# The second layer's residual gate, spread over the partitions by a DRAM round trip instead of products on TensorE

## The chip, the cores and the metric

The kernel runs on one core of one Trainium2 chip. The metric is device time in microseconds (us) of one execution of the whole program, the median of several runs. The program is one launch; all weights, both token streams and the small parameters come from DRAM, and the output goes back there.

## The reference, cut to what matters

The model has two layers. Each normalises its tokens, multiplies them into one wide input projection that feeds three mixers (a state-space scan, differential attention, a matrix-memory LSTM), merges the three branches by sigmoid gates and projects the sum back. What the change touches is the last line of a layer: the residual gate, one number per channel that does not depend on the token.

```
shift, scale, gate = jnp.split(jax.nn.silu(c) @ w_mod + b_mod, 3, axis=-1)
...
mixed = (g[..., 0, :] * (ya @ w_branch[0]) + g[..., 1, :] * (yb @ w_branch[1])
         + g[..., 2, :] * (yc @ w_branch[2]))
return mixed @ w_out
...
x_new = x + gate[:, None] * merge(y_a, y_b, y_c, p[13])
xc_new = xc + gate_c * merge(yc_a, yc_b, yc_c, pc[13])
```

D_MODEL is 1024, and there are 256 latent tokens and 256 context tokens. The last layer has only the latent tokens to finish, since only they are returned.

## The kernel before, in words

Tokens lie on the 128 partitions in the output stage (a tile is 128 tokens by channels), so the gate must be there on every partition: the tile `gbc`, 128 x 1024. But the modulation is computed with channels on the partitions: `modc[l]` is 128 x 24 x 2, where column 16 + k of a stream holds the gate's channels 128k to 128k + 127. The kernel turns the one into the other on TensorE: for each k it takes the column `modc[l][:, 16 + k, cc]`, repeats it 128 times along the free axis as the stationary operand, and multiplies it with the identity `ident` (line 1269). The result in PSUM (`pm`, 128 x 128 for each k) is the row of 128 gate values on all partitions. ScalarE copies it out of PSUM with a factor 0.5 (line 1271). That is 8 products and 2 copies for a stream; the first layer does it for two streams, the last for one. Each of these products is two passes on TensorE, as they are float32, and so shows as two rows in the trace.

All large products are split in two parts, high and low, and computed as three products. A piece of weights (a granule, 128 x 1024, `raw`) is loaded by SP's queue (line 128), its high part `whi` is cast on ScalarE (line 117), its low part `wlo` is the difference on VectorE (line 83, by the helper `tt`), and 24 products per accumulator follow on TensorE (lines 146 to 148 with tokens on the output's partitions, lines 177 to 179 with channels there). `raw`, `whi` and `wlo` have three buffers each. A load can start when VectorE has made the `wlo` of the granule three before it, and a cast when TensorE has left the buffer of the granule three before.

The merge of a layer goes branch by branch (line 1218). The branch's result is transposed (line 1212), scaled and split in `yh` (ScalarE, line 92) and `yl` (VectorE, line 80), and then for each of four blocks of 256 channels a gate projection (`hh`, `hl`) and a branch projection (`yh`, `yl`) are computed. The third branch's result `yc` is finished late: the LSTM's last head is scaled by `riC`, which comes from a sum of squares through two small operations on GpSimd (`rs_p`, lines 89 and 83, the function `rsqrt`) and one on VectorE (line 87), and then multiplied in on VectorE (`yc`, line 80). After the merge the output projection runs: two blocks whose weights are split as above, and two whose weights were split early in the idle tiles of `yh` and `yl` (lines 1313 to 1321). The result times `gbc` is added to the residual (lines 1292 and 1293).

The second layer's modulation is computed in the first layer's merge (`mod_steps`, called from line 1199). Its last part, the gate columns, is written to `modc` by VectorE at the end of that merge (line 238).

The order of the work is set by a scheduler that works through the program by priority. `band(0)` is the most urgent (loads, splits and evacuations), then `band(1)`, then `band(2)` (the large products). SP issues its loads strictly in the order that results; so does each engine with its instructions, and an instruction that waits holds all behind it.

Of the kernel before, what the change touches and what calls it, by code (L numbers as in the profile page):

```python
# [14 lines left out]
ALU = mybir.AluOpType  # L15
# [3 lines left out]
D = 1024  # L19
P = 128  # L20
# [14 lines left out]
def hybrid_backbone_kernel(ctx: ExitStack, tc: tile.TileContext, A, out, dbg=None):  # L35
    nc = tc.nc
    V, S, G, T = nc.vector, nc.scalar, nc.gpsimd, nc.tensor
# [5 lines left out]
    @contextmanager  # L43
    def band(b):
        saved = tc.cur_priority
        tc.cur_priority = bands[b]
        yield
        bands[b] = tc.cur_priority
        tc.cur_priority = saved
# [3 lines left out]
    rows_d = ctx.enter_context(tc.tile_pool(name="rows_d", bufs=1, space=bass.MemoryType.DRAM))  # L53

    def mk(pool, shape, tag, dt=F32, bufs=1):
        if dbg is not None:
            b = 1
            for n in shape[1:]:
                b *= n
            b *= 2 if dt == BF16 else 4  # L60
            key = (pool.name, tag)
            dbg["usage"][key] = max(dbg["usage"].get(key, 0), (b + 31) // 32 * 32 * bufs)
        return pool.tile(list(shape), dt, tag=tag, name=tag, bufs=bufs)
# [4 lines left out]
    def pe():  # L68
        return mk(psum, [P, 512], "pe", bufs=PE_)

    def pm():
        return mk(psum, [P, 512], "pm", bufs=PM)
# [12 lines left out]
    def tsc(o, a, s1, op0, s2=None, op1=None, eng=None):  # L85
        if op1 is None:
            (eng or V).tensor_scalar(out=o, in0=a, scalar1=s1, scalar2=None, op0=op0)
        else:
            (eng or V).tensor_scalar(out=o, in0=a, scalar1=s1, scalar2=s2, op0=op0, op1=op1)
# [17 lines left out]
    modc = [mk(base, [P, 24, 2], "modc", bufs=2) for _ in range(depth)]  # L107
# [113 lines left out]
    def mod_mm(ps, x, k0, wm):  # L221
        for j in range(2):
            k = k0 + j
            g = k % 4

            T.matmul(
                ps[32 * g : 32 * g + 32, :], lhsT=cst[:, k, 2 - 2 * x : 34 - 2 * x], rhs=wm[:, j, :],
                start=(x == 0 and k < 4), stop=(x == 1 and k >= 4), skip_group_check=True,
            )

    def mod_tail(l, cbs, row):
        with band(2):
            pc = pacc()
            for i in range(4):
                T.matmul(pc[:, 4 * i : 4 * i + 4], lhsT=row[:, i * P : (i + 1) * P], rhs=selm, start=True, stop=True)
            for x, cb in enumerate(cbs):
                r = 16 * l + 12 + cb // 3
                tt(
                    modc[l][:, cb * 4 : cb * 4 + 4, :], pc[:, 0:16].rearrange("p (a b) -> p a b", b=4)[:, :, 2 * x : 2 * x + 2],
                    bc(pcols[:, 4 * (cb % 3) : 4 * (cb % 3) + 4, r], 2), ALU.add,  # L240
                )
# [24 lines left out]
    def mod_steps(l, cbs, pool):  # L266

        ps = None
        for x, cb in enumerate(cbs):
            with band(2):  # L270
                ps = ps or pe()
                for k0 in range(0, KT, 2):
                    wm = mk(pool, [P, 2, 512], "wm", bufs=4)
                    with band(0):
                        nc.sync.dma_start(
                            wm, A["w_mod"][l][k0 * P : (k0 + 2) * P, cb * 512 : (cb + 1) * 512].rearrange("(k p) n -> p k n", p=P)
                        )
                    mod_mm(ps, x, k0, wm)
                if x:
                    row = mk(pool, [P, 512], "modrow", bufs=1)  # L280
                    S.copy(row, ps)
            yield
        mod_tail(l, cbs, row)
        yield
# [157 lines left out]
    for l in range(depth):  # L442
        last = l == depth - 1
# [753 lines left out]
        bg = tc.alloc_tile_pool(name=f"bg{l}", bufs=1)  # L1197
        later = ([] if l else [(0, (4, 5))]) + ([] if last else [(l + 1, (c, c + 1)) for c in (0, 2, 4)])
        steps = chain.from_iterable(mod_steps(*x, bg) for x in later)
        mixed = []  # L1200
        mT = ([], [])
        per = D // nqt
# [58 lines left out]
        with band(1):  # L1261
            gbc = {}
            for p in pq:
                gbc[p] = mk(ep, [P, D], "gbc", bufs=2)
                cc = 1 - p
                for hf in range(2):
                    pt = pm()
                    for k in range(4):
                        T.matmul(chunk(pt, k), lhsT=modc[l][:, 16 + 4 * hf + k, cc : cc + 1].to_broadcast([P, P]), rhs=ident, start=True, stop=True)

                    S.mul(gbc[p][:, hf * 512 : (hf + 1) * 512], pt, 0.5)
            if l == 0:
                for p in pq:
                    for i in range(2):
                        for g in range(2):
                            src = (A["x"] if p else A["ctx"])[0][i * P : (i + 1) * P, g * 512 : (g + 1) * 512]
                            nc.sync.dma_start(xnew.tile(g, 2 * p + i), src)
# [114 lines left out]
```

## Time and profile before

| what | value |
|---|---|
| runs | 1692.8, 1693.22 and 1695.64 us, median 1693.22 |
| profiled execution | 1696.51 us, its span (first to last instruction) 1694.7 us |
| TensorE (PE) busy | 1651.4 us, 97% of the span |
| VectorE (DVE) busy | 1098.4 us, 65% |
| ScalarE (ACT) busy | 767.4 us, 45% |
| GpSimd (POOL) busy | 188.3 us, 11% |
| DMA, from HBM | 193.03 MB, 115 GB/s over the span |
| mean granted TensorE clock | 0.992 |

A row of the timeline gives the start, the time taken, engine, line, operation and tiles of an instruction, and in brackets how long its engine was idle before it and what ended that. Lines are those of the kernel before. SPq is SP's queue, which issues the loads. A row of the windows gives for one stretch how long each engine was busy, the granted clock, the share of the DMA engines' time that was used and the rate at which they moved bytes.

### The profile page before, as it was taken

What the parts mean: (1) busy time and instruction counts of PE and PEld (TensorE: products, weight loads), DVE (VectorE), ACT (ScalarE), POOL (GpSimd) and SP (SyncE); (2) the same over time, 40 slices, a digit from 0 to 9 for tenths busy, and PEclk for the clock granted to TensorE, in tenths of its full rate; (3) what the DMA queues carried; (4) which work ended last, traced back from release to release, by engine and by line L of the source; (5) the groups of instructions that cost most, each with busy time, mean ns of one, the idle gap of its engine ahead of it and who ended that gap; (6) DMA issues with size and microseconds to landing.
All of it is one profiled execution on the core that took longest, in us unless ns stands there. A gap on an engine that the chain in (4) does not pass through costs nothing. (4 is left out here: it accounts for less than half of the span.)

```text
span 1694.7 us, 28789 instructions
## 1 busy us (share of the span) xinstructions
PE 1651.4 (97%) x11288; PEld 1472.5 (87%) x11288; DVE 1098.4 (65%) x2183; ACT 767.4 (45%) x1497; POOL 188.3 (11%) x232
## 2 busy tenths in 40 slices
PE   5999999999999899999999999999999999999998
PEld 2797899999898899977777789987899999999998
DVE  4797688676874677622334354887877867775565
ACT  3446744554544443422223233535545555444453
POOL 0103513100100000000010001011221111000100
PEclk8999999999999999999999999999999999999999
DMA  8544532222222222353544542334342334335654
GB/s 263 127 117 129 147 88 73 68 74 63 77 63 67 84 88 64 128 179 96 185 134 128 161 139 54 100 106 130 108 125 76 100 88 128 109 112 164 185 168 145
DMA packets 203332, 196.48 MB, mean 116 GB/s; under 512 B 21790, under 2 KB 183968, under 8 KB 203196
## 3 DMA queue, kind: packets, MB, share of 16 engines
q1 hardware_dynamic: 203196, 194.64, 39.5%
q8 instruction: 89, 1.46, 0.3%
q14 instruction: 47, 0.39, 0.1%
HBM read 193.03 MB, written 1.57 MB: 115 GB/s over the span
## 5 line engine op out<-in xcount | busy, mean ns | idle before, releaser
L83 DVE TENSOR_TENSOR wlo<-raw,whi 128x1024 fp32r<-128x1024 f32 x274 | 352.0, 1285 | 307.0 <-ACT whi L117 304.6
L146 PE MATMUL acc<-whi,hh 128*128 128x256 f32 x1728 | 504.7, 292 | 6.9 <-DVE zz L80 5.4
L147 PE MATMUL acc<-wlo,hh 128*128 128x256 f32 x1728 | 504.4, 292 | 0.0
L148 PE MATMUL acc<-whi,hl 128*128 128x256 f32 x1728 | 502.3, 291 | 0.0
L117 ACT CAST whi<-raw 128x1024 fp32r<-128x1024 f32 x274 | 287.2, 1049 | 388.5 <-PE acc L178 251.4
L146 PEld LDWEIGHTS acc<-whi,hh 128*128 128x128 f32 x1728 | 331.2, 192 | 19.6 <-issue 9.4
L147 PEld LDWEIGHTS acc<-wlo,hh 128*128 128x128 f32 x1728 | 331.5, 192 | 13.1 <-issue 10.8
L148 PEld LDWEIGHTS acc<-whi,hl 128*128 128x128 f32 x1728 | 331.2, 192 | 10.8 <-issue 8.7
L177 PE MATMUL acc<-hh,whi 128*128 128x512 f32 (+1 forms) x712 | 252.7, 357 | 1.5 <-DVE cv_a L80 1.5
L178 PE MATMUL acc<-hl,whi 128*128 128x512 f32 (+1 forms) x712 | 253.8, 357 | 0.1
L179 PE MATMUL acc<-hh,wlo 128*128 128x512 f32 (+1 forms) x712 | 251.9, 355 | 0.0
L177 PEld LDWEIGHTS acc<-hh,whi 128*128 128x128 f32 x712 | 134.2, 189 | 29.0 <-issue 7.8
L179 PEld LDWEIGHTS acc<-hh,wlo 128*128 128x128 f32 x712 | 134.5, 189 | 19.2 <-issue 1.4
L178 PEld LDWEIGHTS acc<-hl,whi 128*128 128x128 f32 x712 | 134.6, 189 | 18.8 <-issue 1.7
L178 PE MATMUL acc<-yl,whi 128*128 128x512 f32 (+1 forms) x384 | 128.6, 337 | 0.0
L177 PE MATMUL acc<-yh,whi 128*128 128x512 f32 (+1 forms) x384 | 128.4, 338 | 0.0
L179 PE MATMUL acc<-yh,wlo 128*128 128x512 f32 (+1 forms) x384 | 127.8, 336 | 0.0
L945 ACT ACTIVATE E<-pe,nmax 128x512 f32<-128x512 f32 (+1 forms) x96 | 58.8, 617 | 45.2 <-DVE nmax L943 43.4
L178 PEld LDWEIGHTS acc<-yl,whi 128*128 128x128 f32 x384 | 72.1, 188 | 8.0
L179 PEld LDWEIGHTS acc<-yh,wlo 128*128 128x128 f32 x384 | 71.8, 188 | 8.3
L177 PEld LDWEIGHTS acc<-yh,whi 128*128 128x128 f32 x384 | 71.9, 188 | 7.3
L789 ACT ACTIVATE ex<-ex,col 128x128 f32<-128x128 f32 x192 | 60.7, 392 | 29.2 <-POOL ex L744 29.2
(300 smaller groups left out, 2431.0 us busy)
## 6 DMA issues: line engine op xcount, KB each, us to landing
raw<-in_w_in_dram SPq DMA_DIRECT2D x192, 512.0 KB
raw<-in_w_branch_dram SPq DMA_DIRECT2D x48, 512.0 KB
wm<-in_w_mod_dram SPq DMA_DIRECT2D x45, 512.0 KB
raw<-in_w_in_dram SPq DMA_DIRECT2D x48, 256.0 KB
ex<-acs_d SPq DMA_DIRECT2D x32, 256.0 KB
raw<-in_w_out_dram SPq DMA_DIRECT2D x16, 512.0 KB
ex<-acs_d SPq DMA_DIRECT2D x32, 128.0 KB
pw<-nm_d SPq DMA_DIRECT2D x8, 256.0 KB
```

Of the source, the lines that this page charges most:

```text
L83: (eng or V).tensor_tensor(out=o, in0=a, in1=b, op=op)
L117: S.copy(hi, raw)
L146: T.matmul(o, lhsT=xh[:, k, sl], rhs=hi[:, j, :], start=(k == 0 and i == 0), stop=False)
L147: T.matmul(o, lhsT=xh[:, k, sl], rhs=lo[:, j, :], start=False, stop=False)
L148: T.matmul(o, lhsT=xl[:, k, sl], rhs=hi[:, j, :], start=False, stop=(k == KT - 1 and i == 1))
L177: T.matmul(o, lhsT=hi[:, j, cs], rhs=xh[:, k, a:b], start=(k == 0 and first), stop=False)
L178: T.matmul(o, lhsT=hi[:, j, cs], rhs=xl[:, k, a:b], start=False, stop=False)
L179: T.matmul(o, lhsT=lo[:, j, cs], rhs=xh[:, k, a:b], start=False, stop=(k == KT - 1 and final))
L789: S.activation(ex[:, c, :], ex[:, c, :], AF.Exp, bias=col[:, LDT, c, d, h : h + 1])
L945: S.activation(e_, o, AF.Exp, bias=ng[:, m : m + 1], accum_out=rs[:, m : m + 1])
```

## The change

In the last layer the gate goes through DRAM. Ahead of the merge, and with the most urgent priority, the eight columns of `modc` are written to a DRAM tile `gate_d` of 1024 numbers. In the output stage one DMA reads `gate_d` back on all 128 partitions (each partition gets the same 4 KB), and GpSimd multiplies the result by 0.5 in place. The products with the identity and the two copies on ScalarE go away in the last layer; the first layer keeps them.

```
@@ -1197,6 +1197,10 @@
         bg = tc.alloc_tile_pool(name=f"bg{l}", bufs=1)
         later = ([] if l else [(0, (4, 5))]) + ([] if last else [(l + 1, (c, c + 1)) for c in (0, 2, 4)])
         steps = chain.from_iterable(mod_steps(*x, bg) for x in later)
+        if last:
+            gate_d = mk(rows_d, [D], "gate_d")
+            with band(0):
+                nc.sync.dma_start(gate_d.rearrange("(k p) -> p k", p=P), modc[l][:, 16:24, 0])
         mixed = []
         mT = ([], [])
         per = D // nqt
@@ -1263,6 +1267,12 @@
             for p in pq:
                 gbc[p] = mk(ep, [P, D], "gbc", bufs=2)
                 cc = 1 - p
+                if last:
+
+                    with band(0):
+                        nc.sync.dma_start(gbc[p], gate_d.partition_broadcast(P))
+                    tsc(gbc[p], gbc[p], 0.5, ALU.mult, eng=G)
+                    continue
                 for hf in range(2):
                     pt = pm()
                     for k in range(4):
```

How the change moves instructions, at three places. In the changed kernel the lines behind the first insertion count 4 more, and those behind the second 10 more.

The first place is SP's queue at the end of the first layer, where the weights of the output projection are loaded (`raw` from `w_out`, lines 128 and 1319). Before:

```order
L1277 DMA y<-in_x_dram 128x512 x2
L128 DMA raw<-in_w_out_dram 128x4x256 x2
L1319 DMA raw<-in_w_out_dram 128x4x256 x3
L1277 DMA y<-in_x_dram 128x512 x2
L1319 DMA raw<-in_w_out_dram 128x4x256
L128 DMA raw<-in_w_in_dram 128x4x128 x2
```

And in the changed kernel:

```order
L1287 DMA y<-in_x_dram 128x512 x2
L128 DMA raw<-in_w_out_dram 128x4x256 x2
L1329 DMA raw<-in_w_out_dram 128x4x256
L1203 DMA gate_d<-modc 128x8x1
L1329 DMA raw<-in_w_out_dram 128x4x256 x2
L1287 DMA y<-in_x_dram 128x512 x2
L1329 DMA raw<-in_w_out_dram 128x4x256
L128 DMA raw<-in_w_in_dram 128x4x128 x2
```

The write of the gate, 1024 pieces of 4 bytes, now stands ahead of the second of four early loads of `w_out`. It waits for VectorE's write of the gate columns of `modc`.

The second place is SP's queue at the start of the last layer's merge. Before:

```order
L742 DMA pw<-nm_d 128x256
L128 DMA raw<-in_w_in_dram 128x4x256 x7
L128 DMA raw<-in_w_branch_dram 128x4x256 x2
L128 DMA raw<-in_w_in_dram 128x4x256 x2
L128 DMA raw<-in_w_branch_dram 128x4x256 x2
```

And in the changed kernel:

```order
L742 DMA pw<-nm_d 128x256
L128 DMA raw<-in_w_in_dram 128x4x256 x7
L128 DMA raw<-in_w_branch_dram 128x4x256 x2
L128 DMA raw<-in_w_in_dram 128x4x256
L1273 DMA gbc<-gate_d 128x1024
L128 DMA raw<-in_w_in_dram 128x4x256
L128 DMA raw<-in_w_branch_dram 128x4x256 x2
```

The broadcast read stands between the two loads of the second gate block. It waits for the LSTM's last product with the carried state (line 1094), as `gbc` takes memory that the LSTM's tiles held.

The third place is GpSimd and VectorE shortly behind that. On GpSimd the last rows of the program before are these:

```order
L89 TENSOR_SCALAR rs_p<-ssC 128x2
L83 TENSOR_TENSOR rs_p<-rs_p,mhalf 128x2
L89 TENSOR_SCALAR rs_p<-ssC 128x2
L83 TENSOR_TENSOR rs_p<-rs_p,mhalf 128x2
L83 TENSOR_TENSOR y<-y,tg 128x256 x8
```

And in the changed kernel:

```order
L89 TENSOR_SCALAR rs_p<-ssC 128x2
L83 TENSOR_TENSOR rs_p<-rs_p,mhalf 128x2
L87 TENSOR_SCALAR gbc<-gbc 128x1024
L89 TENSOR_SCALAR rs_p<-ssC 128x2
L83 TENSOR_TENSOR rs_p<-rs_p,mhalf 128x2
L83 TENSOR_TENSOR y<-y,tg 128x256 x8
```

The multiplication by 0.5 stands ahead of the last pair of `rs_p`, which makes the last head's `riC`. On VectorE the same stretch reads, before:

```order
L80 SCALAR_TENSOR_TENSOR yl<-pe,pcols,yh 128x256 x2
L87 TENSOR_SCALAR riC<-rs_p 128x2
L80 SCALAR_TENSOR_TENSOR yc<-yc,riC,zz 128x256 x2
L83 TENSOR_TENSOR wlo<-raw,whi 128x1024
L80 SCALAR_TENSOR_TENSOR yl<-pm,pcols,yh 128x256
L80 SCALAR_TENSOR_TENSOR yl<-pe,pcols,yh 128x256
L80 SCALAR_TENSOR_TENSOR yl<-pm,pcols,yh 128x256
L83 TENSOR_TENSOR wlo<-raw,whi 128x1024
```

And in the changed kernel:

```order
L80 SCALAR_TENSOR_TENSOR yl<-pe,pcols,yh 128x256 x2
L83 TENSOR_TENSOR wlo<-raw,whi 128x1024
L80 SCALAR_TENSOR_TENSOR yl<-pm,pcols,yh 128x256
L87 TENSOR_SCALAR riC<-rs_p 128x2
L80 SCALAR_TENSOR_TENSOR yl<-pe,pcols,yh 128x256
L80 SCALAR_TENSOR_TENSOR yl<-pm,pcols,yh 128x256
L80 SCALAR_TENSOR_TENSOR yc<-yc,riC,zz 128x256 x2
L83 TENSOR_TENSOR wlo<-raw,whi 128x1024
```

`riC` and the two multiplications of `yc` moved behind the next `wlo`, so that `wlo` no longer stands behind GpSimd's result. On TensorE the products of line 1269 are gone in the last layer, and some products of neighbouring blocks change places with each other; nothing else is added or left out there.

## Rows read from the trace of the kernel before

**Rows 1.** Windows: busy time of each engine by stretch, clock, DMA share, GB/s.

```profile
1040.00:1060.00 20.00, 18.01 (x138) 17.21 (x137) 11.26 (x25) 9.15 (x23) 7.56 (x16) 0.91 0.00 1
...
1500.00:1560.00 60.00, 60.00 (x485) 59.17 (x484) 41.56 (x84) 28.79 (x51) 2.14 (x4) 1.00 0.51 150
...
1620.00:1690.00 70.00, 69.97 (x589) 69.76 (x587) 42.32 (x60) 30.61 (x47) 0.28 (x1) 1.00 0.53 162
```

**Rows 2.** The chain that ended last, 1560 us to the end: pieces with L1269.

```profile
1628.16 0.89 PE pm L1269 x8
...
1630.47 0.89 PE pm L1269 x8
```

**Rows 3.** Groups by line, 1560 us to the end, of what goes away, and one ACT row.

```profile
L117 ACT CAST whi<-raw 128x1024 fp32r<-128x1024 f32 x38 | 39.9, 1049 | 54.3 <-PE acc L178 49.1 <-issue 4.4 <-ACT tg L1226 0.7
...
L1271 ACT ACTIVATE gbc<-pm 128x512 f32<-128x512 f32 x2 | 1.2, 600 | 1.8 <-PE pm L1269 1.7
```

**Rows 4.** Timeline at the end of the first layer, DVE and SPq, where the write will stand.

```profile
1001.76 0.24 DVE L83 TENSOR_TENSOR modc<-acc,pcols 128x8 f32<-128x8 f32 x2
1001.92 1.22 DVE L83 TENSOR_TENSOR wlo<-raw,whi 128x1024 fp32r<-128x1024 f32 x1
...
1003.16 2.10 SPq L1319 DMA_DIRECT2D raw<-in_w_out_dram  x2
...
1014.13 4.71 SPq L540 DMA_DIRECT2D raw<-in_w_in_dram  x6
```

**Rows 5.** Timeline, ACT, DVE and PE: the splits behind those loads, and their use.

```profile
1011.81 1.22 DVE L83 TENSOR_TENSOR wlo<-raw,whi 128x1024 fp32r<-128x1024 f32 x1
...
1022.97 2.00 ACT L117 CAST whi<-raw 128x1024 fp32r<-128x1024 f32 x2 [9.31 <-DMA raw<-in_w_in_dram]
...
1026.09 0.28 PE L146 MATMUL acc<-yh,yb 128*128 128x256 f32 x1
```

**Rows 6.** Timeline, PE and SPq: the last product of line 1094, and the next load.

```profile
1524.15 0.59 PE L1094 MATMUL pe<-C,uq 128*128 128x257 f32 x2
...
1524.83 0.37 SPq L128 DMA_DIRECT2D raw<-in_w_in_dram  x1
```

**Rows 7.** Windows of 2 us: the stretch in which that load moved.

```profile
1526.00:1528.00 2.00, 2.00 (x19) 2.00 (x19) 1.89 (x4) 1.68 (x4) 0.00 (x0) 1.00 0.86 255
```

**Rows 8.** Timeline, SPq and POOL: a small broadcast read, and its user.

```profile
1447.15 0.34 SPq L742 DMA_DIRECT2D pw<-nm_d  x1
...
1450.13 0.87 POOL L744 TENSOR_SCALAR_AFFINE_SELECT pw<-pw 128x256 f32<-128x256 f32 x1 [8.85 <-DMA pw<-nm_d]
```

**Rows 9.** One tile's instructions (hh): POOL's product with a scalar, duration min/median/max.

```profile
L89 POOL TENSOR_SCALAR hh<-hf x32: 402/438/981, 33.5 to 1062.0; 128x256 fp32r<-128x256 f32 x32
```

**Rows 10.** Timeline, POOL: the last pair of rs_p.

```profile
1529.71 0.19 POOL L89 TENSOR_SCALAR rs_p<-ssC 128x2 f32<-128x2 f32 x1 [23.88 <-ACT sq L1138]
1529.99 0.70 POOL L83 TENSOR_TENSOR rs_p<-rs_p,mhalf 128x2 f32<-128x2 f32 x1
```

**Rows 11.** Timeline, ACT and DVE, 1530 to 1536 us.

```profile
1530.13 1.07 ACT L117 CAST whi<-raw 128x1024 fp32r<-128x1024 f32 x1
1533.28 1.05 ACT L117 CAST whi<-raw 128x1024 fp32r<-128x1024 f32 x1 [0.69 <-PE acc L178]
...
1530.93 0.88 DVE L80 SCALAR_TENSOR_TENSOR yc<-yc,riC,zz 128x256 f32<-128x256 f32 x2
1531.72 1.22 DVE L83 TENSOR_TENSOR wlo<-raw,whi 128x1024 fp32r<-128x1024 f32 x1
1532.86 0.48 DVE L80 SCALAR_TENSOR_TENSOR yl<-pm,pcols,yh 128x256 fp32r<-128x256 f32 x1
```

**Rows 12.** Timeline, PE: first products with the low parts of the next two granules of hh.

```profile
1533.90 0.28 PE L179 MATMUL acc<-hh,wlo 128*128 128x256 f32 x1
...
1538.60 0.29 PE L179 MATMUL acc<-hh,wlo 128*128 128x256 f32 x1
```

**Rows 13.** Timeline, DVE: a wlo that began beside POOL's work on y.

```profile
1596.96 1.57 DVE L83 TENSOR_TENSOR wlo<-raw,whi 128x1024 fp32r<-128x1024 f32 x1 [0.54 <-ACT whi L117]
```

More of the change, by code (lines that the diff above doesn't have):

```diff
@@ L1199, in hybrid_backbone_kernel @@
         steps = chain.from_iterable(mod_steps(*x, bg) for x in later)
+        if last:
+            gate_d = mk(rows_d, [D], "gate_d")
+            with band(0):
+                nc.sync.dma_start(gate_d.rearrange("(k p) -> p k", p=P), modc[l][:, 16:24, 0])
         mixed = []
@@ L1265, in hybrid_backbone_kernel @@
                 cc = 1 - p
+                if last:
+                    with band(0):
+                        nc.sync.dma_start(gbc[p], gate_d.partition_broadcast(P))
+                    tsc(gbc[p], gbc[p], 0.5, ALU.mult, eng=G)
+                    continue
                 for hf in range(2):
```

## The prediction

> **What bounds the kernel now.** I read the windows first, then the chain of waits, then the timelines of the places at which the order changes. The windows say that TensorE does not pause in the second layer's last 190 us: busy 60.00 of 60 us and 69.97 of 70 at a granted clock of 1.00, with VectorE and ScalarE well below [rows 1]. The products that the change removes lie in that stretch, and the chain that ended last runs through them: two pieces of L1269 with 0.89 us each [rows 2]. These are the 8 products of the layer, 16 passes. ScalarE's casts of weights, in turn, are idle mostly until TensorE leaves a buffer (49.1 of 54.3 us), not until a load lands [rows 3]. So TensorE sets the pace there, and what is taken from its stream should reach the end. The numbers below are made against the profiled execution (1696.51 us, span 1694.7), which is 3.3 us above the median of the runs, 1693.22. I take the same difference off the median.
>
> **The products that go.** Two pieces of 0.89 us on the chain [rows 2] are 1.78 us. They are followed by products at the usual pace and nothing waits for them but ScalarE's two copies (1.2 us in all [rows 3]), which lie beside TensorE's work and give nothing. The bounds are 0, if TensorE waited instead, and 1.78; I take 1.78, because behind them TensorE had no gap in which the time could vanish [rows 1].
>
> **The write of the gate.** On SP it stands between the first and the second early load of w_out and waits for the gate columns, which VectorE finishes at 1001.76 + 0.24 = 1002.0 us. The load behind it went out at 1003.16, as soon as VectorE had made the wlo of 1001.92 + 1.22 = 1003.14 [rows 4]. No row shows such a write. The nearest are the six loads of L540, each made of 1024 small pieces (128 x 8, 16 or 64 bytes): SP took 4.71 us to issue six, 0.79 us each [rows 4]. So the write would be issued by 1002.8, before the next load could go: nothing on SP. On the DMA engines the same six bound it from above, whatever their own cost is: from the first issue (1014.13) to the cast that waited for them (1022.97) is 8.8 us [rows 4, 5]. From below it costs nothing; a gain is excluded, as it is only added work. I take the 0.8 us. What would be late is the split of w_out behind it: the last granule's wlo is ready at 1011.81 + 1.22 = 1013.03, and TensorE needs it 48 products of 0.118 us (5.7 us) before 1026.09, thus at 1020.4 [rows 5]. That is 7.4 us of cover. At 0.8 us the cost is nothing, at the upper end 8.8 - 7.4 = 1.4 us.
>
> The Trainium skill speaks against this write: "DMA: Bandwidth & Descriptors", Rules for kernel authors, says that an access whose last dimension is not contiguous becomes one descriptor per element, and that it should be rearranged. By that rule the write is 1024 transfers of 4 bytes, as I counted. The rows of L540 agree in kind, and the sum stays the same as long as the cover holds.
>
> **The read on 128 partitions.** On SP it waits for the last product of line 1094, which ends at 1524.15 + 0.59 = 1524.74. The load behind it went out at 1524.83 before [rows 6], so it holds that load by one issue, some 0.4 us. It moves 128 times 4 KB, 512 KB like the load itself, and the load moved within 1526 to 1528 at 255 GB/s, so the read takes about 2 us [rows 7]. From below, it lands at 1528.0 like that load; from above, a small read of this kind (128 KB) had its user start 3.0 us after its issue [rows 8], and 384 KB more at 255 GB/s are 1.5 us, thus 1524.8 + 4.5 = 1529.3. I take 1528.4. The load behind is then 2.4 us late; its cast came at 1533.28 and waited for TensorE's buffer [rows 11], some 5 us after it had landed, so nothing follows.
>
> **The product by 0.5 on GpSimd.** A product of 128 x 256 with a scalar took 0.438 us there, 0.981 at most [rows 9]; four times that is 1.75 us, 3.9 at most, and 1.6 by the shortest. It would run from 1528.4 to 1530.2. Behind it in GpSimd's queue stands the last pair of rs_p, which began at 1529.71 and ended at 1530.69 before [rows 10]; it would end at 1531.1. Who waits for it is VectorE's riC. In the new order a wlo stands ahead of riC: it starts when the cast of 1530.13 + 1.07 ends, at 1531.2, and ends at 1532.4, and riC follows one more yl later, at about 1532.8. GpSimd is 1.7 us early there, so nothing. This wlo itself ended at 1531.72 + 1.22 = 1532.94 before and was used at 1533.90 [rows 11, 12], the smallest margin of the stretch, 0.96 us; it now ends earlier, and its margin grows to 1.5.
>
> **The sum.** 1.78 us off, and nothing added on the path: 1694.7 for an execution like the profiled one, 1693.22 - 1.78 = 1691.4 for the median, or 0.11%. A measurement of this kernel can tell about 0.2%, 3.4 us, from no change. I expect less than that.
>
> **Rivals.** First, GpSimd and VectorE get in each other's way. A wlo that began while GpSimd worked on y took 1.57 us instead of 1.22 [rows 11, 13]. If the read lands 1 to 2 us later than I think, the product by 0.5 runs beside the wlo of 1531.2, and if that wlo had to stand aside for all of 1.75 us, it would end at 1534.2, 0.3 us too late for 1533.90. Time: 1691.7. For it speaks that this is the tightest place, against it that 0.3 is the worst. The Trainium skill, "SBUF — State Buffer", Who interferes with whom, has the rule: a VectorE instruction with two inputs in SBUF contends with a GpSimd instruction that reads SBUF, and the later one is fully blocked. The trace agrees with the rule in direction, with the 0.35 us longer wlo.
>
> Second, TensorE waits for something else once the products are gone, since casts and loads do not come earlier with it. Then up to all of the 1.78 us is given back, 1691.4 to 1693.2; I set 1693.0. Against it: the casts wait for TensorE's buffers [rows 3], so they come earlier too.
>
> Third, the write delays w_out by its upper bound: 1.4 us lost, 1692.8.
>
> Fourth, and on the other side, the read lands late and VectorE stands at riC. If it lands at T, riC can start at T + 1.75 + 0.98. From rs_p's end to the first yc were 0.24 us with riC in it, then come in the new order two yl (0.48 each), the two yc (0.88) and a wlo (1.22) [rows 10, 11], so that wlo ends at T + 6.0. TensorE uses it at 1538.60 [rows 12]. It decides from T = 1532.6, 7.8 us after the issue, on. A pause costs more than itself: in the stretch of 1040 to 1060, in which TensorE paused 2 us, the granted clock was 0.91 on the mean, part of it at 1.2 instead of 2.4 GHz, and 0.09 x 20 = 1.8 us of full speed were lost [rows 1]. The saving is gone and 3.4 us more are lost when the wait is 3.4 us (1.78 + 3.4 - 1.8), that is at T = 1536.0, 11 us after the issue. At T = 1537 the time is 1691.4 + 4.4 + 1.8 = 1697.6. For it: all 128 pieces read the same 4 KB of DRAM, and no row shows that at this size. Against it: the small broadcast took 3 us in all [rows 8].
>
> **How the numbers follow.** Forecast 0.78; first rival 0.07, second 0.05, third 0.04, fourth 0.04; 0.02 for a gain from the moved products that no row shows. The runs before spread from 1692.8 to 1695.64, so a median of few runs may come out 1 us off; 1691.4 less 1.6 us is already faster by 0.2% (below 1689.8), and slower begins at 1696.6. From the cases and this scatter: faster 0.10, same 0.84, slower 0.06. The range takes in the forecast with the scatter and the second and third rival: 1689.7 to 1694.0. It leaves out the fourth.
>
> **What would show it.** Right: the rows of the gate's products are gone from the second layer; TensorE stays busy for all of 1500 to 1690; the last product ends about 1.8 us earlier; the write is issued before 1003 and the loads behind it go out at the same times; GpSimd's product by 0.5 starts about 1528 and takes 1.6 to 1.8 us; riC finds rs_p done. Wrong: a wait of TensorE for wlo or yl near 1534, with a lower clock behind it; an idle VectorE ahead of riC; casts in the first layer's end that wait longer for w_out; a gap in TensorE behind 1628. A time outside 1689.8 to 1696.6 would say that an effect of the order or of the DMA queue is larger than every term here.

## The result, and the profile after

The changed kernel takes 1701.62 us (median of 5 runs, 1700.33 to 1704.68) against 1693.12 for the kernel before on the same chip (5 runs, 1689.91 to 1695.64): a ratio of 1.0056, 95% interval 1.0045 to 1.0066. It is slower by 8.5 us, where 1.8 us less was forecast. The profiled execution took 1703.55 us, span 1701.7; that is 7.0 us above the profiled execution before, where the medians differ by 8.5.

I compared the two traces by the start of the same VectorE instruction in both. At 961 us the changed kernel is 1.2 us ahead, before it has done anything new. Between 1002 and 1024 us (the end of the first layer) it falls from 1.2 us ahead to 6.6 behind, between 1145 and 1199 from 7.0 to 8.9 behind, and at the removed products it wins some back. Counted from the 1.2 us ahead, the profile thus loses 8.2 us. The last step first, in the timelines of VectorE: two wlo of the second layer, before and after.

```profile
1591.30 1.22 DVE L83 TENSOR_TENSOR wlo<-raw,whi 128x1024 fp32r<-128x1024 f32 x1 [0.94 <-ACT whi L117]
...
1639.45 1.23 DVE L83 TENSOR_TENSOR wlo<-raw,whi 128x1024 fp32r<-128x1024 f32 x1 [0.94 <-ACT whi L117]
```

```profile
1600.17 1.22 DVE L83 TENSOR_TENSOR wlo<-raw,whi 128x1024 fp32r<-128x1024 f32 x1 [0.94 <-ACT whi L117]
...
1646.53 1.23 DVE L83 TENSOR_TENSOR wlo<-raw,whi 128x1024 fp32r<-128x1024 f32 x1 [0.22 <-ACT whi L117]
```

The first is 8.87 us late, the second, behind the place of the products, 7.08. The 1.79 us between them are the saving, and TensorE is as full there as it was [rows 1]. The windows of the changed kernel (busy time of PE, PEld, DVE, ACT, POOL, then clock, DMA share, GB/s):

```profile
1500.00:1560.00 60.00, 60.00 (x477) 58.82 (x476) 43.20 (x93) 28.25 (x51) 5.46 (x5) 1.00 0.50 149
...
1620.00:1690.00 70.00, 70.00 (x591) 70.00 (x590) 45.60 (x63) 34.48 (x51) 1.44 (x2) 1.00 0.59 179
```

The loss begins at the write. SP's timeline of the changed kernel:

```profile
1000.81 0.37 SPq L1203 DMA_DIRECT2D gate_d<-modc  x1
1001.94 2.10 SPq L1329 DMA_DIRECT2D raw<-in_w_out_dram  x2
```

SP lost nothing: the write was out in 0.37 us, and the load behind it left 1.2 us ahead of its time in [rows 4], as everything did. But the data did not come. Windows of 2 us, of before (first fence) and of the changed kernel (second); the last two columns are the DMA share and GB/s.

```profile
1004.00:1006.00 2.00, 2.00 (x19) 2.00 (x18) 1.47 (x2) 0.39 (x1) 0.00 (x0) 1.00 0.83 258
1006.00:1008.00 2.00, 2.00 (x20) 2.00 (x19) 0.18 (x1) 1.26 (x2) 0.00 (x0) 1.00 0.91 262
```

```profile
1002.00:1004.00 2.00, 2.00 (x19) 2.00 (x18) 2.00 (x3) 1.17 (x3) 0.00 (x0) 1.00 0.20 18
1004.00:1006.00 2.00, 2.00 (x20) 2.00 (x19) 0.25 (x1) 0.00 (x0) 0.00 (x0) 1.00 0.04 7
1006.00:1008.00 2.00, 2.00 (x19) 2.00 (x19) 0.00 (x0) 0.00 (x0) 0.00 (x0) 1.00 0.35 52
1008.00:1010.00 2.00, 2.00 (x19) 2.00 (x18) 0.00 (x0) 0.00 (x0) 0.00 (x0) 1.00 0.38 25
1010.00:1012.00 2.00, 2.00 (x19) 2.00 (x18) 0.00 (x0) 0.00 (x0) 0.00 (x0) 1.00 0.39 31
1012.00:1014.00 2.00, 2.00 (x19) 2.00 (x18) 0.00 (x0) 0.00 (x0) 0.00 (x0) 1.00 0.78 215
```

The loads were issued by 1004.0, and for 8 us behind that the core's DMA engines move 7 to 52 GB/s. Then the rate is normal again. ScalarE from 1004 and VectorE from 1006 us on stand idle (0.00 in their columns), ScalarE at a cast that needs the load and VectorE at the split behind that cast. TensorE still works on what it has. Next, the timelines of ACT, DVE and PE of the changed kernel, and then the same `yh` and `otmp` of before:

```profile
1014.52 1.05 ACT L117 CAST yh<-raw 128x1024 fp32r<-128x1024 f32 x1 [11.36 <-DMA raw<-in_w_out_dram]
...
1015.60 1.23 DVE L83 TENSOR_TENSOR yl<-raw,yh 128x1024 fp32r<-128x1024 f32 x1 [11.35 <-ACT yh L117]
1018.33 1.23 DVE L83 TENSOR_TENSOR yl<-raw,yh 128x1024 fp32r<-128x1024 f32 x1 [1.50 <-ACT yh L117]
1019.48 1.22 DVE L83 TENSOR_TENSOR wlo<-raw,whi 128x1024 fp32r<-128x1024 f32 x1
1020.86 0.91 DVE L537 MEMSET raw<- 128x1024 f32 x1 [0.16 <-DVE wlo L83]
1021.68 0.63 DVE L83 TENSOR_TENSOR otmp<-acc,gbc 128x512 f32<-128x512 f32 x1
...
1022.37 0.58 PE L146 MATMUL acc<-whi,yb 128*128 128x256 f32 x1 [5.81 <-DVE otmp L83]
```

```profile
1006.74 1.05 ACT L117 CAST yh<-raw 128x1024 fp32r<-128x1024 f32 x1 [2.35 <-DMA raw<-in_w_out_dram]
...
1014.02 0.63 DVE L83 TENSOR_TENSOR otmp<-acc,gbc 128x512 f32<-128x512 f32 x1
```

`otmp` (in evac_out) empties an accumulator of TensorE; there are three. It needs nothing from the late loads, but it stands on VectorE behind two yl that do, and behind a wlo whose own load was issued ahead of the write, but whose cast stands on ScalarE behind the casts of the late loads. From the load's issue to `yh` it was 3.6 us before (1003.16 to 1006.74) and is 12.6 now: the loads are held up by 9.0 us. `otmp` is late by 8.9 (7.66, and the 1.2 that the kernel was ahead). TensorE waits 5.8, so the evacuation had a cover of 3.1 us. What the pause costs on top stands in the clock column:

```profile
1020.00:1022.00 2.00, 0.00 (x0) 0.00 (x0) 1.84 (x3) 1.04 (x1) 0.00 (x0) 0.50 0.11 9
1022.00:1024.00 2.00, 1.63 (x7) 1.63 (x8) 2.00 (x4) 0.00 (x0) 0.00 (x0) 0.50 1.05 268
1024.00:1026.00 2.00, 2.00 (x12) 2.00 (x11) 1.33 (x3) 0.00 (x0) 0.00 (x0) 0.50 0.90 68
1026.00:1028.00 2.00, 2.00 (x16) 2.00 (x16) 0.00 (x0) 0.00 (x0) 0.00 (x0) 0.85 0.56 16
```

While TensorE stood still its granted clock fell to 0.50 (1.2 of 2.4 GHz). It worked at that level from 1022.4 to about 1026.6, so 4.2 us gave 2.1 us of work. 5.8 + 2.1 = 7.9 us, which is the whole step at this place (from 1.2 ahead to 6.6 behind, to 0.1).

That leaves the 1.9 us between 1145 and 1199 us. TensorE's longest waits from 1150 on are those of before (1.2 us for xw and 0.9 for cv_a, there 1.2 and 1.0). But the clock fell behind them in this profile, and in the one before it did not (changed kernel first, then before):

```profile
1155.00:1170.00 15.00, 12.83 (x43) 8.55 (x43) 11.46 (x18) 8.03 (x16) 1.22 (x2) 0.89 0.42 101
```

```profile
1155.00:1170.00 15.00, 12.87 (x56) 8.76 (x55) 14.93 (x25) 6.19 (x8) 1.14 (x1) 1.00 0.26 72
```

0.11 x 15 = 1.7 us of the 1.9. Whether this belongs to the change, the runs below do not settle.

### The profile page after: what moved, and what is told of

It reads as the page before. It is cut to its first block, busy times and chain, and to the rows that moved or that the text cites. A ratio compares the mean times of both kernels' runs of the same rounds, so it can differ in the third digit from the quotient of the medians.

```text
span 1701.7 us, 28760 instructions
## 1 busy us (share of the span) xinstructions
PE 1651.8 (97%) x11272; PEld 1471.6 (86%) x11272; DVE 1096.2 (64%) x2183; ACT 766.0 (45%) x1495; POOL 191.7 (11%) x233
## 5 line engine op out<-in xcount | busy, mean ns | idle before, releaser
L146 PE MATMUL acc<-whi,hh 128*128 128x256 f32 x1728 | 503.8, 292 | 5.4 <-DVE zz L80 5.3
L146 PEld LDWEIGHTS acc<-whi,hh 128*128 128x128 f32 x1728 | 330.4, 191 | 18.2 <-issue 9.4
```

What stands on the lines that cost most here:

```text
L146: T.matmul(o, lhsT=xh[:, k, sl], rhs=hi[:, j, :], start=(k == 0 and i == 0), stop=False)
```

## The experiments

The times are medians, each with the ratio to the kernel before on the same chip (which came out at 1692.71 to 1693.12 there). "Load to cast" is the time, in the run's timelines, from the issue of the load behind the write to the first cast of it. "TensorE waits" is the row "PE acc L146 <- DVE otmp" at the first layer's end.

| kernel | us | ratio, 95% interval | load to cast, us | TensorE waits, us |
|---|---|---|---|---|
| before | 1693.12 | 1 | 3.6 | 0 |
| changed | 1701.62 | 1.0056 (1.0045 to 1.0066) | 12.6 | 5.8 |
| write alone | 1700.81 | 1.0042 (1.0029 to 1.0055) | 12.3 | 5.4 |
| read alone | 1691.14 | 0.9983 (0.9975 to 0.9992) | no write | 0 |
| changed, splits on GpSimd | 1694.39 | 1.0004 (0.9995 to 1.0013) | other order | 0.6 |
| before, splits on GpSimd | 1693.97 | 1.0005 (0.9997 to 1.0014) | no write | 0 |
| changed, write by GpSimd's queue | 1700.06 | 1.0051 (1.0038 to 1.0064) | 12.8 | 5.2 |
| 1024 pieces of 4 bytes, read | 1693.48 | 1.0005 (0.9997 to 1.0014) | no write | 0 |
| 128 pieces of 32 bytes | 1692.88 | 1.0000 (0.9991 to 1.0008) | 3.7 | 0 |
| 512 pieces of 4 bytes | 1701.90 | 1.0055 (1.0042 to 1.0067) | 12.0 | 4.9 |
| 128 pieces of 4 bytes | 1699.38 | 1.0037 (1.0024 to 1.0049) | 10.1 | 3.1 |
| 1024 pieces, 512 bytes apart | 1693.02 | 1.0006 (0.9997 to 1.0015) | 4.6 | 0 |
| 1024 pieces, 64 bytes apart | 1692.70 | 0.9995 (0.9986 to 1.0004) | 4.5 | 0 |
| changed, write in the second layer | 1691.56 | 0.9991 (0.9982 to 1.0000) | elsewhere | 0 |
| changed, write of 8 rows | 1690.18 | 0.9985 (0.9977 to 0.9994) | elsewhere | 0 |

**The two halves apart.** The kernel before with the write only; nothing reads it, and the products stay.

```diff
+        if last:
+            gate_d = mk(rows_d, [D], "gate_d")
+            with band(0):
+                nc.sync.dma_start(gate_d.rearrange("(k p) -> p k", p=P), modc[l][:, 16:24, 0])
```

> The kernel before with the gate's write added and read by nobody; the second layer's products stay. Theory A (the write of 1024 four-byte pieces to DRAM delays the loads of w_out behind it in the DMA queue, VectorE stands at their splits, and TensorE waits for the accumulator behind them): the whole loss without the gain, about 9 us slower than before, 1702; a wait of TensorE for otmp of 5 to 6 us near 1016 and a lower granted clock behind it. Theory B (the loss comes with the broadcast read or with GpSimd's product by 0.5): no change, 1693.

And the changed kernel without the write, its read taking other 4 KB of DRAM:

```diff
-                        nc.sync.dma_start(gbc[p], gate_d.partition_broadcast(P))
+                        nc.sync.dma_start(gbc[p], A["b_mod"][l, 2 * D : 3 * D].partition_broadcast(P))
```

> The changed kernel without the write: the broadcast read takes 4 KB of the bias b_mod in place of the gate, so the gate's value is left out of the residual. Theory A: the saved 1.78 us alone, about 1691.4, with TensorE busy through 1500 to 1690. Theory B: as slow as the changed kernel, 1701.

The write alone costs 8.0 us against its own before (1692.79), with the same wait in the waits view of TensorE:

```profile
PE acc L146 <- DVE otmp L83: 5.4, 1, 5.4
```

The read alone gains 1.65 (2.9 by its ratio). So the saving is real and the loss is the write's. The two do not quite add up to the change: by the medians their sum is 6.4 us lost where the changed kernel loses 8.5, by the ratios 4.2 where it loses 9.5. The second difference, 5.2 us, is more than the errors of the three ratios make (some 3 us together), so it is not shown to be chance. Part of it can be the write-alone kernel itself, of which there are 4 runs: with only 512 pieces (below) the write alone lost 9.2 us. Another part has the place of the stretch at 1155 to 1170 us. In the write-alone profile the clock is 1.00 there, and from 1100 to 1210 us that kernel gains 1.6 us on before; with 512 pieces it loses 0.1. The clock falls there in two of the 15 profiles, the changed kernel's and that of the changed kernel with the splits on GpSimd (next run):

```profile
1155.00:1170.00 15.00, 12.89 (x51) 9.25 (x50) 14.34 (x22) 5.51 (x8) 1.04 (x1) 0.89 0.23 71
```

With the write issued by GpSimd's queue, otherwise the changed kernel, it is 1.00, and that kernel wins 0.4 us between 1145 and 1199. The profile before has waits of the same length at a clock of 1.00. I leave these 2 to 5 us open.

**VectorE's order.** In the changed kernel the first layer's early splits of w_out, their casts on ScalarE and their differences on VectorE, go to GpSimd, so that `otmp` no longer stands behind them.

```diff
-                    split(raw, wh[ix], wl[ix])
+                    if last:
+                        split(raw, wh[ix], wl[ix])
+                    else:
+                        tsc(wh[ix], raw, 1.0, ALU.mult, 0.0, ALU.add, eng=G)
+                        tt(wl[ix], raw, wh[ix].bitcast(F32), ALU.subtract, eng=G)
```

> The changed kernel, with the four early splits of w_out in the first layer made on GpSimd instead of ScalarE and VectorE, so that nothing that waits for the late loads stands ahead of otmp. Theory A: the write still delays the loads by 9 to 11 us, but TensorE no longer waits for otmp; 1691 to 1695, depending on whether GpSimd finishes the splits before their use. Rival C (TensorE waits because the accumulator or the weights are late for another reason that the write causes): still 1699 to 1702.

Its control is the same edit in the kernel before:

> Control for the run in which the four early splits of the first layer's w_out stand on GpSimd: the same move in the kernel before, without the write. If the move itself costs nothing, 1693 us, and that run's 1694.4 would hold the saving of 1.8 us and a loss of about 3 us that the write still causes. If the move costs, by slower splits on GpSimd, as much as is missing there, about 1695.5 to 1696 us, and the write then costs nothing once VectorE is free of the splits.

The loads are held up as in the changed kernel with this edit too: its DMA engines move 26 to 38 GB/s from 1004 to 1010 us. The first `otmp` is on time all the same, and TensorE pauses for 0.6 us:

```profile
1010.55 0.63 DVE L83 TENSOR_TENSOR otmp<-acc,gbc 128x512 f32<-128x512 f32 x1
...
1014.03 1.05 POOL L89 TENSOR_SCALAR yh<-raw 128x1024 fp32r<-128x1024 f32 x1 [10.74 <-DMA raw<-in_w_out_dram]
```

The changed kernel gains 7.2 us by it, the kernel before loses 0.8 by its ratio, within its error. So it was the order on ScalarE and VectorE that carried the late loads to TensorE; the edit frees both at once, so it does not tell them apart. With the saving the edit should have reached 1692.2 (1693.97 - 1.78), and 2.2 us are still missing by the medians, 1.6 by the ratios, each known to about 1.5 us. In its profile 1.4 us are lost between 1002 and 1060 us, of which the wait shows 0.6, and 2.0 between 1145 and 1210, where its clock fell as shown above.

**What holds up the loads.** First the queue. The write is issued from GpSimd's queue:

```diff
-                nc.sync.dma_start(gate_d.rearrange("(k p) -> p k", p=P), modc[l][:, 16:24, 0])
+                nc.gpsimd.dma_start(gate_d.rearrange("(k p) -> p k", p=P), modc[l][:, 16:24, 0])
```

> The changed kernel, with the write of 1024 four-byte pieces issued from GpSimd's queue rather than SyncE's, at the same place. Theory Q (order within one queue: the loads stand behind the small writes on SyncE's queue): the loads of w_out move at once, the first split of the late granules starts within 4 us of the first layer's last gate column, no wait of TensorE for the evacuation, about 1691.2 us. Theory M (the memory or the DMA engines are held by the small writes, whatever queue issues them): the loads are late as in the changed kernel, about 1701 us.

It is theory M. The load is issued at 998.24 and its cast starts at 1011.01, and the row of the write in the list of DMA issues gives its time to landing, 11.2 us:

```profile
gate_d<-modc POOLq DMA_DIRECT2D x1, 4.0 KB, 11.2
```

The Trainium skill says in "DMA: Bandwidth & Descriptors", Issuing engines are not separate DMA queues, that starting transfers from several engines saves only the sequencer's time. This run agrees: another issuer, the same hold-up (12.8 us from load to cast).

Then the direction: the same 1024 pieces, read.

```diff
+        if last:
+            gl = mk(small, [P, 8], "gl")
+            with band(0):
+                V.tensor_copy(gl, modc[l][:, 16:24, 0])
+                nc.sync.dma_start(gl, A["w_out"][l, 0:8, 0:P].rearrange("k p -> p k"))
```

> The kernel before, plus a dead transfer in the place of the write, in the other direction: 1024 pieces of 4 bytes read from DRAM into a tile of 128 x 8 that nothing reads. Theory D (the direction: small pieces written to DRAM hold up the loads behind them, read ones do not): the 24576 four-byte pieces of the six narrow loads of the first layer's end were issued and landed in about 5 us, so 1024 cost about 0.2 to 0.8 us, hidden; 1693 us, TensorE no longer than 0.5 us without work between 1010 and 1030 us, DMA traffic above 200 GB/s within 4 us of the issue. Theory C (the number of pieces, in either direction): as with the write, about 1700 to 1701 us with TensorE 5 us without work.

Theory D: no wait of TensorE. The load behind the pieces was issued at 1003.59 and cast at 1009.74 us, 6.2 us later; before, the same load took 4.7 us (1004.90 to 1009.59), so the hold-up is 1.5 us. (The traffic stayed at 102 to 141 GB/s for the first 6 us, not above the 200 expected, and TensorE waited for none of it. The six narrow loads are not 24576 pieces of 4 bytes, as the expectation has it, but 6144 of 16 or 64 bytes.)

Then the size and the number of pieces. These edits are in the kernel before, as dead writes at the same place: 128 pieces of 32 bytes, and 512 of 4.

```diff
...
+                nc.sync.dma_start(gate_d.rearrange("(p k) -> p k", p=P), modc[l][:, 16:20, :].rearrange("p a b -> p (a b)"))
```

> The kernel before, plus a dead write at the place of the changed kernel's: the same 128 partitions and about the same place in the program, but 128 pieces of 32 bytes (1024 values, 4 KB) in place of 1024 of 4 bytes. Theory C (the hold-up grows with the number of pieces): 128/1024 of about 11 us, 1.4 us, inside the cover of about 3 us that the accumulator's evacuation has; about 1693 us. Theory F (a fixed hold-up for any write of pieces under some size): about 1700 us with TensorE 5 us without work.

```diff
...
+                nc.sync.dma_start(gate_d[0:512].rearrange("(k p) -> p k", p=P), modc[l][:, 16:20, 0])
```

> The kernel before, plus a dead write of half the columns at the same place: 512 pieces of 4 bytes. Theory C (the hold-up grows with the number of pieces written): half of the 11 us, about 5.5 us, less the evacuation's cover of about 3 us: TensorE 2 to 3 us without work between 1010 and 1030 us, 1695 to 1697 us. Theory F (fixed by the first small write, whatever their number): as with 1024 pieces, about 1700.8 us.

The 32-byte pieces cost nothing, as theory C wanted, but half the 4-byte pieces held the loads up nearly as long as all of them (12.0 us from load to cast) and cost no less time, so C falls. F falls by the 32-byte pieces. The idea left was the place in DRAM: in the 4-byte writes, partition p's piece lies beside that of partition p+1, 128 in a row of 512 bytes. So I spread them out, and then wrote one such row alone.

```diff
...
+            gate_d = mk(rows_d, [D, P], "gate_d")
...
+                nc.sync.dma_start(gate_d[:, 0].rearrange("(k p) -> p k", p=P), modc[l][:, 16:24, 0])
```

> The kernel before, plus the dead write of all 1024 pieces of 4 bytes at the same place, but each piece 512 bytes from the next in DRAM instead of beside it. Theory N (the hold-up comes from pieces of different partitions that land beside each other, in the same stretch of DRAM): nothing to hold up, about 1693 us, TensorE less than 0.5 us without work there. Theory C (the number of pieces, wherever they land): about 1700.8 us with TensorE 5 us without work.

```diff
...
+            gate_d = mk(rows_d, [D, 16], "gate_d")
...
+                nc.sync.dma_start(gate_d[:, 0].rearrange("(k p) -> p k", p=P), modc[l][:, 16:24, 0])
```

> The kernel before, plus the dead write of all 1024 pieces of 4 bytes at the same place, each piece 64 bytes from the next in DRAM. Theory R with the row of 512 bytes as its unit: 8 pieces to a row in place of 128, so about 0.7 us, hidden; 1693 us. If spacing under 512 bytes is not enough: above 1697 us, with a wait of TensorE for the evacuation.

```diff
...
+                nc.sync.dma_start(gate_d[0:P].rearrange("(k p) -> p k", p=P), modc[l][:, 16:17, 0])
```

> The kernel before, plus a dead write of one column of the gate at the same place: 128 pieces of 4 bytes side by side, 512 bytes of DRAM in all. Theory R (what counts is how many pieces land side by side in one row of 512 bytes, worked off one after the other while the rows go beside each other: 128 in the runs with 1024 and with 512 pieces): the loads are held up by about 11 us again, TensorE about 5 us without work, 1700 to 1702 us. Theory S (several rows at once, or more than 128 pieces, are needed): about 1693 us, and TensorE without such a wait.

Windows of three kernels, some 4 us behind the write's issue (at 997.67, 999.94 and 998.35 us): 1024 pieces 512 bytes apart, 1024 pieces 64 bytes apart, and 128 pieces side by side.

```profile
1002.00:1004.00 2.00, 2.00 (x20) 2.00 (x19) 0.00 (x0) 0.63 (x1) 0.00 (x0) 1.00 0.86 279
```

```profile
1004.00:1006.00 2.00, 2.00 (x20) 2.00 (x20) 0.00 (x0) 0.46 (x1) 0.00 (x0) 1.00 0.88 296
```

```profile
1002.00:1004.00 2.00, 2.00 (x21) 2.00 (x19) 0.00 (x0) 0.00 (x0) 0.00 (x0) 1.00 0.11 37
1004.00:1006.00 2.00, 2.00 (x19) 2.00 (x18) 0.00 (x0) 0.00 (x0) 0.00 (x0) 1.00 0.56 32
```

1024 pieces that lie 64 bytes apart let the loads pass at 296 GB/s, and 128 that touch hold them at 32 to 37. The single row costs 6.5 us from load to cast (10.1 - 3.6), the 512 and 1024 pieces 8.4 and 8.7. That is theory R, with a remainder: one row gives three quarters of the hold-up, not all of it, and the kernel's time (1699.38, its wait of 3.1 us) lies just under the range that R gave.

The Trainium skill gives a size in "DMA: Bandwidth & Descriptors", Specifications: transfers below 512 bytes make the DMA engines read, modify and write. By that alone the pieces 64 bytes apart and those of 32 bytes should have cost too; they held the load up by 0.9 and 0.1 us, and the kernel's time did not change. Whether such a cycle is what the neighbouring pieces wait for, no run here shows. Nor do the runs show how near two pieces must lie: nothing was run with pieces of 4 bytes between 4 and 64 bytes apart.

**The same write elsewhere.** The changed kernel, with the write at the start of the second layer, where no load follows for some 12 us. Two small VectorE instructions halve the columns first, so GpSimd's halving is gone.

```diff
+                gate_d = mk(rows_d, [D], "gate_d")
+                gate_s = mk(small, [P, KT], "gate_s")
+                tsc(gate_s, xn[3][:, 0:KT], 0.0, ALU.mult)
+                stt(gate_s, modc[l][:, 16:24, 0], 0.5, gate_s, ALU.mult, ALU.add)
+                nc.sync.dma_start(gate_d.rearrange("(k p) -> p k", p=P), gate_s)
...
```

> The changed kernel, with the same write of 1024 four-byte pieces moved to the start of the second layer, behind its fifth w_in load, where SyncE issues nothing until about 1076 us and the DMA share is 0.01 (the columns are halved by VectorE first, two instructions of 128 x 8, so that GpSimd's halving is gone). Theory A (only the place of the write costs): the saving alone, about 1691 us, as with the read alone (1691.1). Rival B (the write or the gate's way through DRAM costs wherever it stands): 1694 us or more.

Theory A. Timeline of SP: the write, and the next load 12.5 us behind it.

```profile
1054.42 0.37 SPq L517 DMA_DIRECT2D gate_d<-gate_s  x1
1066.91 15.60 SPq L128 DMA_DIRECT2D raw<-in_w_in_dram  x5
```

**A better form.** The columns are turned into 8 rows by one product with the identity on TensorE and halved by ScalarE on the way; the write is 8 pieces of 512 bytes and stands just ahead of the read, one load between them. GpSimd does nothing.

```diff
...
+                pt = pm()
+                T.transpose(pt[0:KT, 0:P], modc[l][:, 16:24, 0], ident)
+                grow = mk(small, [KT, P], "grow")
+                S.mul(grow, pt[0:KT, 0:P], 0.5)
+            with band(0):
+                nc.sync.dma_start(gate_d, grow)
...
-                        nc.sync.dma_start(gbc[p], gate_d.partition_broadcast(P))
-                    tsc(gbc[p], gbc[p], 0.5, ALU.mult, eng=G)
+                        nc.sync.dma_start(gbc[p], gate_d.rearrange("k p -> (k p)").partition_broadcast(P))
```

> The changed kernel with the gate transposed on TensorE (one product of two passes), halved by ScalarE, and written as 8 contiguous rows of 512 bytes; GpSimd's product goes. Theory A, if the number of pieces or their size is what makes the write slow: no delay of w_out, and 1.78 less about 0.2 us for the transpose, 1691.6. If any write to DRAM ahead of loads holds the queue for 10 us: loads behind it late, and about 1700.

Its write stands at 1519.69 us, so at another place than the changed kernel's, and the run before this one shows that the place alone can take the loss away. But here a load stands right behind the write, issued at 1520.08, and it was not held up:

```profile
1522.00:1524.00 2.00, 2.00 (x20) 2.00 (x18) 2.00 (x4) 2.00 (x8) 0.00 (x0) 1.00 1.04 360
```

Its median, 1690.18 us, is the lowest of all: 2.6 us less than the kernel before in its runs, and 11.4 less than the change as it was made. From the read alone (1691.14), which leaves the gate out, the runs do not tell it apart.

## Why the prediction was wrong

**Right: the products.** 1.78 us were forecast; 1.79 came between 1600 and 1647 us, and TensorE stayed full [rows 1]. The read alone as a kernel gains 1.65.

**Right in the result: the read and GpSimd's product.** The timelines of SP, POOL and DVE in the changed kernel:

```profile
1533.64 0.34 SPq L1273 DMA_DIRECT2D gbc<-gate_d  x1
...
1537.88 2.79 POOL L87 TENSOR_SCALAR gbc<-gbc 128x1024 f32<-128x1024 f32 x1 [23.19 <-DMA gbc<-gate_d]
1540.64 0.73 POOL L89 TENSOR_SCALAR rs_p<-ssC 128x2 f32<-128x2 f32 x1
...
1540.10 1.23 DVE L83 TENSOR_TENSOR wlo<-raw,whi 128x1024 fp32r<-128x1024 f32 x1 [0.64 <-ACT whi L117]
...
1542.22 0.17 DVE L87 TENSOR_SCALAR riC<-rs_p 128x2 f32<-128x2 f32 x1 [0.50 <-POOL rs_p L83]
```

The read had its user start 4.2 us after its issue, where I took 3.6 (4.5 was the upper end). The product took 2.79 us, where I took 1.75 (3.9 was the upper end); it is 2.79 to 2.80 in the other three runs that have it, so four times the product of a quarter of its size was too low. GpSimd was therefore not 1.7 us early at riC: VectorE stood there for 0.50 us. It cost nothing, as TensorE's 60.00 of 60 us show. The fourth rival had its place right and its size wrong. The first rival did not come: the wlo of 1540.10 began while the product still ran (to 1540.67) and took 1.23 us, no longer than elsewhere.

**Wrong: what the write does to the loads.** The step was "The nearest are the six loads of L540", 0.8 us taken and 8.8 as the upper end [rows 4, 5]. Those rows are reads into a tile; this is a write to DRAM. A read of 1024 pieces (run above) holds the load behind it for 1.5 us and costs no time, the write holds the loads for 9.0 us. That the upper end (8.8) came out about right is luck, as its rows are of another kind; what failed is the choice within the bounds, by a row that was near in the number of pieces and not in the direction or in where the pieces land.

**Wrong: the cover.** "That is 7.4 us of cover" was the way from the load to TensorE through the last granule's wlo [rows 5]. It was the wrong way. VectorE works in order, and `otmp`, which needs no load, stood behind the same splits; by it the cover was 3.1 us. The sign that the prediction named for this, casts that wait longer for w_out, is the one that came (11.36 us in place of 2.35). With both the upper end and that cover the third rival would have been 8.8 - 3.1 = 5.7 us of pause, which is what TensorE's row shows (5.81), in place of 1.4.

**Left out: the clock behind the pause.** I priced it for the fourth rival only (1.8 us [rows 1]). Here it was 2.1. 5.7 + 1.8 - 1.78 gives 1693.22 + 5.7 = 1698.9 by the upper end and the right cover. The median is 1701.62, 2.7 us more: 0.4 of it lies in the size of these terms; the rest has about the size of the open stretch behind 1145 us (1.9 in the profile), but that it is the same is not shown.

## What to carry to other kernels

A cover is measured to every instruction that stands behind the late one on its engine, and first to those that empty an accumulator. Looking only at the late data's own use gave 7.4 us here where 3.1 were true. A transfer whose kind and direction no row shows is not priced by a row that agrees in its count alone; if its upper end exceeds any cover, the forecast has to say so with a real chance. A column of 128 partitions that goes to DRAM is better turned first and written in rows: eight pieces of 512 bytes held up nothing in the run, at another place in the program, and 128 neighbouring pieces of 4 bytes held up the loads behind them by 6.5 us. At the same place in the program pieces of 32 bytes, or of 4 bytes that lie 64 bytes apart, cost no time.

## What the runs showed of the hardware that was not expected

Pieces of 4 bytes from neighbouring partitions, written side by side in DRAM, slow the core's transfers to between 7 and 52 GB/s for 8 us, although they come to 4 KB. It does not depend on the issuing queue (12.6 and 12.8 us from load to cast), hardly on their number (12.3, 12.0 and 10.1 us for 1024, 512 and 128), and it is nearly gone when they lie 64 bytes apart (4.5) and gone when they are 32 bytes long (3.7; 3.6 without a write). Which part of the memory or of the DMA engines the loads wait for is not shown.

GpSimd and VectorE slow each other at times. The timelines of VectorE and GpSimd, in the changed kernel with the splits on GpSimd:

```profile
999.68 1.36 DVE L83 TENSOR_TENSOR wlo<-raw,whi 128x1024 fp32r<-128x1024 f32 x1
1000.96 2.87 DVE L83 TENSOR_TENSOR y<-y,tg 128x512 f32<-128x512 f32 x1
...
1000.05 3.23 POOL L83 TENSOR_TENSOR yl<-raw,yh 128x1024 fp32r<-128x1024 f32 x1
```

The addition on VectorE takes 0.68 to 0.69 us otherwise, and the split on GpSimd 2.39 us when it is alone. The ends are near those of three instructions one behind the other: the wlo ends at 1001.04, 2.39 us behind that is 1003.43 (the split ended at 1003.28), and 0.69 behind the split's end is 1003.97 (the addition ended at 1003.83). That each waited for the one begun before it is a reading of this one place. On the other hand the changed kernel's product of 2.79 us ran beside four VectorE instructions of one PSUM operand (0.48 us each, as before [rows 11]) and the start of a wlo (1.23 us) that it did not slow.
